# Four tiles gathered and four computed densely, where it was three and five: a retrieval layer re-split on one Trainium2 core

## The chip, the cores and the metric

The kernel runs on one core of a Trainium2 chip. The metric is the device time of one execution in microseconds (us). The kernel before took 2888.42 us (median of 3 runs, 2881.86 to 2891.72).

## The reference

The input is 1024 tokens of 1024 float32 channels. One layer first mixes tokens (two projections through `w_in` and `w_out`, a short convolution, a spatial gate) and adds the result to the input, giving `h`. Then it retrieves from 16384 single-neuron experts:

```
q    = (rmsnorm(h) @ w_q).reshape(t, 8, 2, 128)            # 8 heads, 2 halves
s    = einsum('thpd,hpkd->thpk', q, sub_keys)              # 128 keys per half
v1, i1 = top_k(s[:, :, 0], 16);  v2, i2 = top_k(s[:, :, 1], 16)
cand = v1[..., :, None] + v2[..., None, :]                 # 16 x 16 sums
cidx = i1[..., :, None] * 128 + i2[..., None, :]
top, pos = top_k(cand, 16);  idx = take(cidx, pos);  gates = softmax(top)
act  = gelu(einsum('thkd,td->thk', expert_u[idx], rmsnorm(h)))
y    = einsum('thk,thkd->td', gates * act, expert_v[idx])  # 8 x 16 experts per token
out  = rmsnorm(h + y)
```

## The kernel before

**Tiles.** The tokens are 8 tiles of 128. Tiles 0 to 3 are group A, tiles 4 to 7 group B. The front (`prep`, `mix`, `query`, `choose`) works on a group at a time. After it, the tiles of `S_TILES` (0, 6, 7) take the sparse path and those of `D_TILES` (1 to 5) the dense path.

**Front.** `mix` streams weight slices of 128 columns (`wide`, L230): each is loaded, split into a rounded part (ACT) and the rest (`split`, L169, on VectorE or one time in three on GpSimd), and multiplied in three products (`mm3`, L182: high by high, high by low, low by high). `query` (L365) does this for the 16 half-heads, and per half-head and tile VectorE searches the 16 largest of 128 scores (`top16`, L474). `choose` (L390) takes, per head, the 50 pairs of ranks that can be among the 16 largest sums (`NCAND`), adds scores on VectorE and indices on GpSimd, searches the 16 largest, and looks their indices up: compare 50 candidates with 16 positions (`eq`, L431, VectorE), multiply by the index (`sel_i`, L433, GpSimd), sum over the candidates (`idx`, L434, VectorE). For group A it is emitted after group B's `mix`; for group B it is interleaved with the queries for two tiles and put into the dense stage for the other two (`LATE`).

**Sparse path** (`sparse`, L510). A slot is one expert rank of one tile: GpSimd issues an indirect DMA that gathers 128 rows of 4 KB (`gx`, L522, 6 buffers), and VectorE consumes it, in a dot product with the token's row (L529) for `peer_u`, or in a multiply-add into `acc` (L538) for `peer_v`. A tile has 128 slots of each kind. It is emitted last and so has the lowest priority; the scheduler that orders each engine's instructions fills it into free time. `pace` (L501) holds it back: from slot `NFREE` = 70 on, each slot comes behind a given mark in VectorE's queue, and the marks are spread over the dense stage.

**Dense path.** `gates` (L549) builds, for each dense token, a 128 x 128 matrix of its gates by expert, from two one-hot matrices per token and a plain fp32 product, and stores it in device memory (`G_dr`). The one-hots are made on VectorE (`o2`, `o1`), the weighing `og` on GpSimd or ACT by the string `OGP`. `dense` (L595) then goes over 128 blocks of 128 experts. `up` multiplies the block's `peer_uT` with the tokens in two halves of 320 (`mm3`), applies Gelu, multiplies by the gates (L634), splits the product into `wh` and `wl` (L637, L638) and splits the block of `peer_v` too (L172, L173). `down` multiplies in three products per tile and half of the channels, over three blocks at a time: for two tiles into persistent PSUM banks, for three into a passing bank that VectorE adds to an accumulator (L651).

**Order.** Each engine runs its queue in order, as the scheduler wrote it. SyncE issues all DMAs but the gathers.

Of the kernel before, what the change touches and what calls it, by code (L numbers as in the profile page):

```python
# [29 lines left out]
NCAND = sum(NB)  # L30

S_TILES = [0, 6, 7]
D_TILES = [1, 2, 3, 4, 5]
GROUPS = [[0, 1, 2, 3], [4, 5, 6, 7]]
# [15 lines left out]
OGB = 2  # L50
O1B = 3
GPER = 3
GLAG = 0
LATE = [range(4, 28, 3), range(29, 61, 4)]
WRB = 2
CTB = 2
N1 = 45
N2 = 69
OGP = "GAAGA"
OGPB = "GA"  # L60
POOL_SPLIT = 1
NFREE = 70
PACE = 0.97


@with_exitstack
def block_kernel(ctx: ExitStack, tc: tile.TileContext, x, attn_g, w_in, conv_w, sgu_wT, sgu_b, sgu_g,
# [21 lines left out]
    dkx = ExitStack()  # L89
    dk = sb(dkx, "dk")  # L90
# [3 lines left out]
    X = [tk.tile([P, KC, 4 * P], F32R, name=n) for n in ("Xh", "Xl")]  # L94

    xt = sb(xtx, "xt")

    class Part:
        def __init__(self, pool, j0, n, late=()):
            self.pool, self.j0, self.n, self.late = pool, j0, n, late  # L100

    class Group:
        def __init__(self, tiles, dest, pool_share):
            self.tiles, self.dest, self.share = tiles, dest, pool_share
            self.nt = len(tiles)
            self.T = self.nt * P
            self.t0 = tiles[0] * P
# [44 lines left out]
    v_.tensor_copy(iota_c, iota_ki[:, 0:NCAND].unsqueeze(2).to_broadcast([P, NCAND, TOPK]))  # L152
# [13 lines left out]
    nsplit = [0]  # L166
    marks = []

    def split(pool, raw, shape, tag, bufs, eng=None):  # L169
# [60 lines left out]
    def wide(G, src, col, rh, rl, order=tuple(range(KC))):  # L230
        wh, wl = wslice(src, col, G.share)
# [5 lines left out]
    def mix(G):  # L237
# [112 lines left out]
        dt = [j for j, t in enumerate(tiles) if t in D_TILES]  # L350
        if dt:
            assert dt == list(range(dt[0], dt[-1] + 1))
            d0 = D_TILES.index(tiles[dt[0]])
            for i in range(2):
                nc.sync.dma_start(hd_dr[i, :, :, d0 * P:(d0 + len(dt)) * P],
                                  G.dest[i][:, :, dt[0] * P:(dt[-1] + 1) * P].bitcast(F32))
        st = [(j, t) for j, t in enumerate(tiles) if t in S_TILES]
        if st:
            gb = tk.tile([P, KC, P], F32, name="wraw", bufs=WRB).rearrange("p k c -> p (k c)")
            nc.sync.dma_start(gb, ffn_g.to_broadcast([P, D]))  # L360
            for j, t in st:
                gp_.tensor_tensor(hs[j], hs[j], gb, ALU.mult)
                nc.sync.dma_start(hn_dr[t * P:(t + 1) * P, :], hs[j])
# [26 lines left out]
    def choose(G, part):  # L390
        nt, late = part.n, part.late
        G, j0, tiles = part, 0, G.tiles[part.j0:part.j0 + part.n]
        for h in range(NH):
            if h:
                yield
            i1 = ks.tile([P, nt, TOPK], F32, name="i1")
            i = a_.activation(i1, G.ti[:, :, 2 * h, :], AF.Copy, scale=128.0)
            if late:
                after(i, marks[late[h]])
            i2 = ks.tile([P, nt, TOPK], F32, name="i2")  # L400
            i = a_.activation(i2, G.ti[:, :, 2 * h + 1, :], AF.Copy)
            if late:
                after(i, marks[late[h]])
            cand = ks.tile([P, nt, NCAND], F32, name="cand")
            cidx = ks.tile([P, nt, NCAND], F32, name="cidx")
            c = 0
            for a0, a1 in ((0, 1), (1, 2), (2, 3), (3, 4), (4, 5), (5, 8), (8, 16)):
                m, n = a1 - a0, NB[a0]
                for eng, dst, first, second in ((v_, cand, G.tv[:, :, 2 * h, :], G.tv[:, :, 2 * h + 1, :]),
                                                (gp_, cidx, i1, i2)):  # L410
                    if n == 1:
                        i = eng.tensor_tensor(dst[:, :, c:c + m], first[:, :, a0:a1],
                                          second[:, :, 0:1].to_broadcast([P, nt, m]), ALU.add)
                    elif m == 1:
                        i = eng.tensor_tensor(dst[:, :, c:c + n], second[:, :, 0:n],
                                          first[:, :, a0:a1].to_broadcast([P, nt, n]), ALU.add)
                    else:
                        i = eng.tensor_tensor(dst[:, :, c:c + m * n].rearrange("p j (a b) -> p j a b", b=n),
                                          second[:, :, 0:n].unsqueeze(2).to_broadcast([P, nt, m, n]),
                                          first[:, :, a0:a1].unsqueeze(3).to_broadcast([P, nt, m, n]), ALU.add)  # L420
                    if late:
                        after(i, marks[late[h]])
                c += m * n
            pos = ks.tile([P, nt, TOPK], U32, name="pos")
            for j in range(nt):
                top16(cand[:, j, :], G.top[:, j0 + j, h, :], pos[:, j, :])
            posf = ks.tile([P, nt, TOPK], BF16, name="posf")
            a_.activation(posf, pos, AF.Copy)
            for j in range(nt):
                eq = ks.tile([P, NCAND, TOPK], BF16, name="eq")  # L430
                v_.tensor_tensor(eq, iota_c, posf[:, j, :].unsqueeze(1).to_broadcast([P, NCAND, TOPK]), ALU.is_equal)  # L431
                sel_i = ks.tile([P, NCAND, TOPK], F32, name="sel_i")
                gp_.tensor_tensor(sel_i, eq, cidx[:, j, :].unsqueeze(2).to_broadcast([P, NCAND, TOPK]), ALU.mult)  # L433
                v_.tensor_reduce(G.idx[:, j0 + j, h, :], sel_i.rearrange("p c k -> p k c"), axis=AX.X, op=ALU.add)  # L434
# [339 lines left out]
```

## Time and profile before

| | |
|---|---|
| median of 3 runs | 2888.42 us |
| span of the profiled execution | 2884.6 us, 3.8 us under that median; the page gives no other time for it |
| TensorE (PE) busy | 2669.2 us, 93% |
| VectorE (DVE) busy | 2447.2 us, 85% |
| GpSimd (POOL) busy | 1422.3 us, 49% |
| ACT busy | 1045.3 us, 36% |
| DMA | 709.93 MB, 246 GB/s over the span |

Durations are of single instructions. Instructions of one engine overlap by their pipelines, so the step from one start to the next is what an engine really takes. The granted clock (PEclk) is a share of 2.4 GHz. The DMA share is the mean busy share of 16 DMA engines.

### The profile page before, as it was taken

The numbers are of one execution on the slowest core, as the hardware profiler recorded it, in microseconds if no ns is written. First come the engines' busy times: TensorE is split into PE (matmuls) and PEld (weight loads), VectorE is DVE, ScalarE is ACT, GpSimd is POOL, SyncE is SP. The second block draws the span as 40 slices with busy tenths as digits, with TensorE's granted clock in tenths as the row PEclk, the third lists the DMA queues.
The fourth block names the chain that finished last, engine by engine and source line by source line (L and its number), as shares of the span: only waits on it lengthen the run. The fifth ranks groups of instructions, "written<-read, shape, count | busy, mean of one in ns | idle before, by whom it ended". The sixth has DMA issues, their size and how long they took to land.

```text
span 2884.6 us, 40045 instructions
## 1 busy us (share of the span) xinstructions
PE 2669.2 (93%) x14243; PEld 2335.5 (81%) x14243; DVE 2447.2 (85%) x4792; ACT 1045.3 (36%) x1973; POOL 1422.3 (49%) x1192
## 2 busy tenths in 40 slices
PE   8997889778885789999999999999999999999998
PEld 6876667567774678888888988999998899899997
DVE  3337979969999869999999999998998888888994
ACT  5224242237765852222323322332323232232223
POOL 0102245644354536766666666655554555554540
PEclk9999978889997889999999999999999999999999
DMA  3225225466446778888889788888888988888881
GB/s 121 81 81 191 74 108 165 154 239 190 128 121 217 223 259 305 312 290 297 309 293 340 284 306 310 316 295 325 323 308 312 331 300 309 316 310 301 308 320 73
DMA packets 270360, 709.93 MB, mean 246 GB/s; under 512 B 21576, under 2 KB 112720, under 8 KB 269904
## 3 DMA queue, kind: packets, MB, share of 16 engines
q0 software_dynamic: 110592, 402.70, 39.7%
q1 hardware_dynamic: 159568, 304.67, 30.7%
q8 instruction: 112, 1.84, 0.3%
q14 instruction: 88, 0.72, 0.1%
HBM read 650.14 MB, written 57.15 MB: 245 GB/s over the span
## 4 chain that ended last, share of the span: by engine, by line
PE 42%; DVE 29%; issue 10%; POOL 6%; DMA 3%; ACT 2%; POOLq 0%; SPq 0%; DVEq 0%; ACTq 0%
PE pu L183 6%; PE pu L184 6%; PE pu L185 6%; DVE gx L529 4%; PE pv L183 4%; PE pv L185 4%; PE pv L184 4%; POOL gx L522 3%; PE pa L184 2%; PE pa L183 2%; PE pa L185 2%; DVE idx L434 2%; POOL sel_i L433 2%; DVE acc L538 2%; DVE a L634 2%
## 5 line engine op out<-in xcount | busy, mean ns | idle before, releaser
L522 POOL DMA_INDIRECT gx<-peer_v,si x384 | 522.8, 1361 | 406.6 <-DVE acc L538 290.3
L522 POOL DMA_INDIRECT gx<-peer_u,si x384 | 497.6, 1296 | 404.5 <-DVE dots L529 257.9
L183 PE MATMUL pu<-hD,uh 128*128 128x320 f32 x2048 | 634.7, 310 | 5.9 <-ACT a L633 5.1
L185 PE MATMUL pu<-hD,ul 128*128 128x320 f32 x2048 | 634.1, 310 | 0.0
L184 PE MATMUL pu<-hD,uh 128*128 128x320 f32 x2048 | 633.9, 310 | 0.0
L529 DVE CUSTOM_DVE_ANT_0 gx<-gx,hn 128x1024 f32<-128x1024 f32 x384 | 478.9, 1267 | 23.4 <-DMA gx<-peer_u,si 23.4
L538 DVE SCALAR_TENSOR_TENSOR acc<-gx,dots,acc 128x1024 f32<-128x1024 f32 x384 | 491.0, 1279 | 5.5 <-DMA gx<-peer_v,si 1.5
L183 PEld LDWEIGHTS pu<-hD,uh 128*128 128x128 f32 x2048 | 385.6, 188 | 9.1 <-ACT a L633 6.4
L184 PEld LDWEIGHTS pu<-hD,uh 128*128 128x128 f32 x2048 | 385.8, 188 | 1.9
L185 PEld LDWEIGHTS pu<-hD,ul 128*128 128x128 f32 x2048 | 385.6, 188 | 0.0
L172 ACT ACTIVATE vh<-raw 128x512 fp32r<-128x512 f32 x256 | 160.9, 633 | 495.5 <-PE pv L185 485.2
L183 PE MATMUL pv<-vh,wh 128*128 128x512 f32 x768 | 304.2, 396 | 27.7 <-DVE ac L651 26.0
L185 PE MATMUL pv<-vh,wl 128*128 128x512 f32 x768 | 302.1, 393 | 3.8 <-DVE wl L638 3.8
L637 ACT ACTIVATE wh<-a 128x320 fp32r<-128x320 f32 x256 | 120.9, 472 | 506.5 <-DVE a L634 493.4
L184 PE MATMUL pv<-vl,wh 128*128 128x512 f32 x768 | 301.1, 392 | 0.0
L185 PE MATMUL pp<-Xh,wl 128*128 128x512 f32 x576 | 242.1, 421 | 20.2 <-DVE wl L173 11.0
L576 PE MATMUL pt<-og,o 128*128 128x128 f32 x1280 | 209.4, 317 | 42.4 <-POOL og L566 25.2
L634 DVE TENSOR_TENSOR a<-a,G 128x320 f32<-128x320 f32 x256 | 186.3, 728 | 72.6 <-ACT a L633 70.8
L183 PE MATMUL pp<-Xh,wh 128*128 128x512 f32 x576 | 242.7, 422 | 3.4 <-ACT wh L172 3.3
L184 PE MATMUL pp<-Xl,wh 128*128 128x512 f32 x576 | 241.8, 420 | 0.0
L576 PEld LDWEIGHTS pt<-og,o 128*128 128x128 f32 x1280 | 184.7, 219 | 68.2 <-POOL og L566 30.0
L173 DVE TENSOR_TENSOR vl<-raw,vh 128x512 fp32r<-128x512 f32 x256 | 173.7, 696 | 41.0 <-ACT vh L172 40.7
(187 smaller groups left out, 4795.0 us busy)
## 6 DMA issues: line engine op xcount, KB each, us to landing
raw<-peer_uT SPq DMA_DIRECT2D x128, 512.0 KB
raw<-peer_v SPq DMA_DIRECT2D x128, 512.0 KB
G_dr<-stg SPq DMA_DIRECT2D x20, 2048.0 KB
G<-G_dr SPq DMA_DIRECT2D x64, 640.0 KB
wraw<-w_in SPq DMA_DIRECT2D x40, 512.0 KB
wraw<-w_q SPq DMA_DIRECT2D x32, 512.0 KB
xt<-x SPq DMA_DIRECT2D x16, 512.0 KB
wraw<-w_out SPq DMA_DIRECT2D x16, 512.0 KB
```

The costliest lines, as they stand in the source:

```text
L172: a_.activation(hi, raw, AF.Copy)
L173: (eng or v_).tensor_tensor(lo, raw, hi.bitcast(F32), ALU.subtract)
L183: pe.matmul(o, lh, rh, start=first, stop=False)
L184: pe.matmul(o, lh, rl, start=False, stop=False)
L185: pe.matmul(o, ll, rh, start=False, stop=last)
L433: gp_.tensor_tensor(sel_i, eq, cidx[:, j, :].unsqueeze(2).to_broadcast([P, NCAND, TOPK]), ALU.mult)
L522: gp_.indirect_dma_start(out=gx, out_offset=None, in_=tab, in_offset=bass.IndirectOffsetOnAxis(ap=ii[:, s:s + 1], axis=0))
L529: pace(v_.tensor_tensor_reduce(gu, gu, hn, 1.0, 0.0, ALU.mult, ALU.add, dots[:, s:s + 1]), slot[0])
L538: pace(v_.scalar_tensor_tensor(acc, gv, dots[:, s:s + 1], acc, op0=ALU.mult, op1=ALU.add), slot[0])
L576: pe.matmul(o[:, i, :], o2[:, m, :], og[:, m, :], start=True, stop=True)
L634: gm = v_.tensor_tensor(a, a, Gt[hf][:, :, c % CB], ALU.mult)
L637: a_.activation(wh[:, sl], a, AF.Copy)
```

## The change

`S_TILES` becomes 0 to 3 (group A) and `D_TILES` 4 to 7 (group B). In detail:

- `choose` is emitted between the queries of its own group, one head behind two half-heads, for A and for B; nothing of it is left for the dense stage. The look-up is split by rank: the first 8 results are looked for among 20 candidates, the other 8 among all 50, for two tiles in one instruction, and the product moves from GpSimd to VectorE. Indices and gates of two heads at a time are handed to the sparse path.
- `NFREE` becomes 150, and the conditions for earlier slots (`N1`, `N2`) go. There are 1024 slots.
- The weight split is always on VectorE. The normalised rows `hn` of tiles 0 to 3 are multiplied on VectorE.
- `gates` runs after all of group B's selection, for 64 blocks of 8 tokens: three of four weigh on ACT, every fourth has VectorE make and weigh `og` in one instruction per token. The first 12 `up`s are emitted between them.
- `up` works on 512 tokens at once and writes Gelu's result into a ring of 4 groups of 4 expert blocks, stored `[P, 512, 4]`; the gates multiply a whole group in one instruction. The result is not split, and `peer_v` is not: `down` is one plain fp32 product per block, tile and half, over 4 blocks. Five of the eight accumulators persist in PSUM, three are `LOOSE`.
- The tokens of group B stay in SBUF (`X`); the copy through `hd_dr` goes.

```diff
-S_TILES = [0, 6, 7]
-D_TILES = [1, 2, 3, 4, 5]
+FIRST = [(0, 1, 0, 8), (1, 2, 0, 4), (2, 4, 0, 2), (4, 8, 0, 1)]
+REST = [(0, 1, 8, 8), (1, 2, 4, 4), (2, 3, 2, 3), (3, 4, 2, 2), (4, 5, 1, 2), (5, 8, 1, 1), (8, 16, 0, 1)]
+S_TILES = [0, 1, 2, 3]
+D_TILES = [4, 5, 6, 7]
-OGP = "GAAGA"
-NFREE = 70
+OGP = "AAAT"
+NFREE = 150
+LOOSE = [(0, 0), (0, 1), (1, 0)]
+ORDER = [(0, 0), (2, 0), (0, 1), (2, 1), (1, 0), (3, 0), (3, 1), (1, 1)]
...
     def choose(G, part):
...
-                gp_.tensor_tensor(sel_i, eq, cidx[:, j, :].unsqueeze(2).to_broadcast([P, NCAND, TOPK]), ALU.mult)
+            for k0, nc_ in ((0, NFIRST), (8, NCAND)):
+                shape = [P, nt, nc_, 8]
...
+                v_.tensor_tensor(eq, iota_c[:, 0:nc_, k0:k0 + 8].unsqueeze(1).to_broadcast(shape),
+                                 posf[:, :, k0:k0 + 8].unsqueeze(2).to_broadcast(shape), ALU.is_equal)
...
+                v_.tensor_tensor(sel, eq, cidx[:, :, 0:nc_].unsqueeze(3).to_broadcast(shape), ALU.mult)
+                v_.tensor_reduce(part.idx[:, :, h, k0:k0 + 8], sel.rearrange("p j c k -> p j k c"), axis=AX.X,
+                                 op=ALU.add)
...
     def gates(pool, tiles, n0, n1, who):
...
+                    for m in range(OB):
+                        v_.tensor_scalar(og[:, m, :], iota_k, d[:, 0, tl + m:tl + m + 1],
+                                         d[:, 2, tl + m:tl + m + 1], op0=ALU.is_equal, op1=ALU.mult)
...
+        def up(self, c, pspool, tag, bufs):
+            g, m = divmod(c, CB)
+            if m == 0:
+                self.ring[g] = self.rp.tile([P, TD, CB], F32, name="ring", bufs=RING)
+            raw = self.up_.tile([P, KC, P], F32, name="uraw", bufs=RB)
+            nc.sync.dma_start(raw, peer_uT[c])
+            uh, ul = split(self.up_, raw, [P, KC, P], "u", 2)
+            o = pspool.tile([P, TD], F32, name=tag, bufs=bufs)
+            for k in range(KC):
+                mm3(o, uh[:, k, :], ul[:, k, :], X[0][:, k, :], X[1][:, k, :], k == 0, k == KC - 1)
+            a_.activation(self.ring[g][:, :, m], o, AF.Gelu)
...
+            for g in range(NG):
+                Gt = pool.tile([P, TD, CB], F32, name="G", bufs=GB)
+                nc.sync.dma_start(Gt, G_dr[:, g, :, :])
+                w = self.ring.pop(g)
+                marks.append(v_.tensor_tensor(w, w, Gt, ALU.mult))
...
+                if g + RING - 1 < NG:
+                    for m in range(CB):
+                        self.up((g + RING - 1) * CB + m, pps, "pu", 2)
+                for j, dh in ORDER:
+                    loose = (j, dh) in LOOSE
+                    o = pps.tile([P, 512], F32, name="pv", bufs=1) if loose else self.accs[j, dh]
+                    for m in range(CB):
+                        pe.matmul(o, w[:, j * P:(j + 1) * P, m], vs[m][:, dh * 512:(dh + 1) * 512],
+                                  start=m == 0 and (loose or g == 0), stop=m == CB - 1 and (loose or g == NG - 1))
+                    if loose:
+                        dst = self.full[j][:, dh * 512:(dh + 1) * 512]
+                        marks.append(v_.tensor_tensor(dst, dst, o, ALU.add))
...
+        qa = query(A, sb(c1, "pqA"))
+        ca = [choose(A, part) for part in A.parts]
+        for h in range(NH):
+            take(qa, 2)
+            for ch in ca:
+                take(ch, 1)
...
+        gg = gates(sb(c1, "gp"), D_TILES, 0, NTB, OGP)
+        for c in range((RING - 1) * CB):
+            dn.up(c, ps, "pp", 4)
+            take(gg, 64 // ((RING - 1) * CB))
```

## Rows read from the trace of the kernel before

**Rows 1.** The page: busy us of each engine, share of the span, instructions.
```profile
PE 2669.2 (93%) x14243; PEld 2335.5 (81%) x14243; DVE 2447.2 (85%) x4792; ACT 1045.3 (36%) x1973; POOL 1422.3 (49%) x1192
```
**Rows 2.** Windows: stretch, its length, busy us by engine, clock, DMA share, GB/s.
```profile
0.00:243.00 243.00, 220.78 (x1004) 176.59 (x1004) 89.04 (x160) 95.83 (x143) 27.18 (x18) 0.94 0.33 104
243.00:366.00 123.00, 106.57 (x494) 86.12 (x494) 119.61 (x627) 40.17 (x70) 31.27 (x48) 0.93 0.36 115
366.00:645.00 279.00, 233.31 (x972) 182.29 (x971) 231.70 (x562) 93.96 (x166) 147.66 (x164) 0.85 0.49 167
645.00:932.00 287.00, 224.28 (x1282) 189.61 (x1280) 268.68 (x877) 187.22 (x412) 131.66 (x111) 0.90 0.54 162
932.00:1046.00 114.00, 90.34 (x512) 77.82 (x512) 91.28 (x83) 90.96 (x198) 62.55 (x28) 0.84 0.73 229
1046.00:1800.00 754.00, 723.47 (x3999) 650.51 (x4000) 696.21 (x1140) 217.17 (x421) 473.56 (x403) 0.99 0.86 304
1800.00:2600.00 800.00, 794.63 (x4454) 722.78 (x4454) 722.56 (x1047) 234.83 (x418) 439.65 (x341) 1.00 0.87 314
```
**Rows 3.** Groups of VectorE instructions: busy us, mean ns, idle before and its releaser.
```profile
L538 DVE SCALAR_TENSOR_TENSOR acc<-gx,dots,acc 128x1024 f32<-128x1024 f32 x384 | 491.0, 1279 | 5.5 <-DMA gx<-peer_v,si 1.5
L529 DVE CUSTOM_DVE_ANT_0 gx<-gx,hn 128x1024 f32<-128x1024 f32 x384 | 478.9, 1267 | 23.4 <-DMA gx<-peer_u,si 23.4
L634 DVE TENSOR_TENSOR a<-a,G 128x320 f32<-128x320 f32 x256 | 186.3, 728 | 72.6 <-ACT a L633 70.8 <-DMA G<-G_dr 1.7
L651 DVE TENSOR_TENSOR ac<-ac,pv 128x512 f32<-128x512 f32 x258 | 175.3, 679 | 12.5 <-PE pv L185 12.5
L173 DVE TENSOR_TENSOR vl<-raw,vh 128x512 fp32r<-128x512 f32 x256 | 173.7, 696 | 41.0 <-ACT vh L172 40.7 <-DMA G_dr<-stg 0.3
L173 DVE TENSOR_TENSOR ul<-raw,uh 128x1024 fp32r<-128x1024 f32 x128 | 157.2, 1228 | 19.3 <-ACT uh L172 19.3
L638 DVE TENSOR_TENSOR wl<-a,wh 128x320 fp32r<-128x320 f32 x256 | 124.1, 485 | 6.7 <-ACT wh L637 6.7
```
**Rows 4.** Timeline of PE in two places: start us, us, instruction, count.
```profile
733.42 3.51 PE L576 MATMUL pt<-og,o 128*128 128x128 f32 x30
...
2000.64 0.39 PE L183 MATMUL pv<-vh,wh 128*128 128x512 f32 x1
...
2016.28 0.31 PE L183 MATMUL pu<-hD,uh 128*128 128x320 f32 x1
...
2019.80 0.31 PE L183 MATMUL pu<-hD,uh 128*128 128x320 f32 x1
```
**Rows 5.** The page's groups: weight loads of the fp32 product, and gathers.
```profile
L576 PEld LDWEIGHTS pt<-og,o 128*128 128x128 f32 x1280 | 184.7, 219 | 68.2 <-POOL og L566 30.0
L522 POOL DMA_INDIRECT gx<-peer_v,si x384 | 522.8, 1361 | 406.6 <-DVE acc L538 290.3
```
**Rows 6.** Timeline of VectorE in the queries: first and last of one half-head's search.
```profile
283.57 0.48 DVE L475 MAX8 tv<-s 128x8 f32<-128x128 f32 x2
...
288.25 1.47 DVE L434 TENSOR_REDUCE idx<-sel_i 128x16 f32<-128x800 f32 x1
```
**Rows 7.** Groups of VectorE in the selection.
```profile
L434 DVE TENSOR_REDUCE idx<-sel_i 128x16 f32<-128x800 f32 x64 | 97.4, 1522 | 40.0 <-POOL sel_i L433 40.0
L431 DVE TENSOR_TENSOR eq<-iota_c,posf 128x800 bf16<-128x800 bf16 x64 | 44.8, 700 | 0.8 <-ACT posf L428 0.8
```
**Rows 8.** Groups of ACT from 932 to 1046 us, where 32 blocks of gates run alone.
```profile
L571 ACT ACTIVATE og<-o,dT 128x128 f32<-128x128 bf16 x128 | 57.7, 519 | 1.0 <-DVE o L561 1.0
L578 ACT ACTIVATE stg<-pt 128x512 f32<-128x512 f32 x64 | 37.8, 591 | 22.0 <-PE pt L576 21.5
```
**Rows 9.** One window of 20 us, columns as in rows 2; and the page's gather queue.
```profile
2460.00:2480.00 20.00, 18.83 (x85) 15.30 (x84) 15.92 (x27) 3.91 (x7) 10.65 (x8) 1.00 1.02 410
...
q0 software_dynamic: 110592, 402.70, 39.7%
```
**Rows 10.** Timeline of VectorE at the end: the last add of a passing bank.
```profile
2871.92 0.69 DVE L651 TENSOR_TENSOR ac<-ac,pv 128x512 f32<-128x512 f32 x1
```

More of the change, by code (lines that the diff above doesn't have):

```diff
@@ L390, in choose @@
     def choose(G, part):
-        nt, late = part.n, part.late
-        G, j0, tiles = part, 0, G.tiles[part.j0:part.j0 + part.n]
-        for h in range(NH):
[L394 to L405, printed above, removed]
+        nt = part.n
@@ L427, in choose @@
[L427 removed]
+                top16(cand[:, j, :], part.top[:, j, h, :], pos[:, j, :])
+            posf = ks.tile([P, nt, TOPK], BF16, name="posf", bufs=2)
             a_.activation(posf, pos, AF.Copy)
[L429 to L432, printed above, removed]
[L433 to L434 removed]
@@ new lines, in choose @@
+            if h % 2:
+                hs = slice(h - 1, h + 1)
+                if sparse_:
+                    for j, t in enumerate(tiles):
+                        v_.tensor_copy(idx_of[t][:, (h - 1) * TOPK:(h + 1) * TOPK].rearrange("p (h k) -> p h k", h=2),
+                                       part.idx[:, j, hs, :])
+                for j in range(nt):
+                    gf, tf = gt[:, j, hs, :], part.top[:, j, hs, :]
+                    v_.tensor_tensor(gf, tf, tf[:, :, 0:1].to_broadcast([P, 2, TOPK]), ALU.subtract)
+                gh = gt[:, :, hs, :]
+                a_.activation(gh, gh, AF.Exp)
+                den = ks.tile([P, nt, 2], F32, name="den", bufs=2)
+                v_.tensor_reduce(den, gh, axis=AX.X, op=ALU.add)
+                v_.reciprocal(den, den)
+                v_.tensor_tensor(gh, gh, den.unsqueeze(3).to_broadcast([P, nt, 2, TOPK]), ALU.mult)
@@ L691, in block_kernel @@
     with ExitStack() as c1:
-        take(query(A, sb(c1, "pqA")))
+        qa = query(A, sb(c1, "pqA"))
[4 more added lines that the diff above has]
+                take(ch, 1)
+        for ch in ca:
+            take(ch)
     load_x(B)
@@ L695, in block_kernel @@
     mix(B)
[L696 to L699 removed]
     xtx.close()
     with ExitStack() as c1:
[L702 to L725 removed]
+        qb = query(B, sb(c1, "pqB"))
+        cb = [choose(B, part) for part in B.parts]
+        for h in range(NH):
+            take(qb, 2)
+            for ch in cb:
+                take(ch, 1)
+        for part, ch in zip(B.parts, cb):
+            take(ch)
+            spread(B, part)
+    tks.close()
+    kdx.close()
+    rx = ExitStack()
+    dn = Dense(sb(rx, "ringp", side="right"), sb(rx, "uvp", side="right"))
+    with ExitStack() as c1:
+        gg = gates(sb(c1, "gp"), D_TILES, 0, NTB, OGP)
+        for c in range((RING - 1) * CB):
+            dn.up(c, ps, "pp", 4)
+            take(gg, 64 // ((RING - 1) * CB))
+        take(gg)
     pre.close()
@@ L730, in block_kernel @@
         pps = c2.enter_context(tc.tile_pool(name="pps", bufs=2, space=PSUM))
-        dense(pool, up_, pacc, pps, D_TILES, hD, u0)
+        dn.run(pool, pacc, pps)
         sparse(spool, S_TILES)
```

362 lines of the change are left out of this document (121 added, 241 removed).

## Prediction

> **What bounds the kernel now.** I read the busy table first, then windows by stage, then the groups and timelines of the stage that is longest. The busy table puts PE at 93% and VectorE at 85% [rows 1], but these are means over different stages [rows 2]. Up to 243 us group A's mixing fills PE; from 243 to 366, in A's queries, VectorE is full (119.6 of 123); from 366 to 645 both are busy with B's mixing and A's selection; from 645 to 932 VectorE again (268.7 of 287), with queries, selection and half of the gates; 932 to 1046 is the rest of the gates. The dense stage runs from 1046 to the end: in its steady part PE is busy 794.6 of 800 us, while the DMA engines are 87% busy at 314 GB/s and VectorE 90%. So the dense stage is bound by PE, the front mostly by VectorE, and the front leaves DMA at 33 to 54%. The change takes PE work out of the dense stage, puts DMA work in, and lengthens the front. Which of these decides is the question.
>
> All sums are made against the profiled span of 2884.6 us, which lies 3.8 us under the median of the runs.
>
> **Up to 243 us.** The weight split leaves GpSimd for VectorE, which is busy 89 of 243 us there; PE is busy 221 [rows 2]. Cost nothing; -10 to +5 us.
>
> **A's queries with selection.** This is now one stretch on VectorE.
> - A search of one half-head over four tiles goes from 283.57 to 288.25, 4.68 us [rows 6]; 16 are 75 us.
> - 16 weight splits at the price of `ul`, 1.23 us [rows 3]: 20 us. Four `hn` products at the same price: 5 us.
> - Selection, per head and pair of tiles, 16 times. The look-up handles 2 x (20 + 50) x 8 = 1120 places, where it was 2 x 800. Compare: 2 x 0.70 x 0.7 = 0.98 us; sum: 2 x 1.52 x 0.7 = 2.13 us [rows 7]; the product, new on VectorE, at the fp32 price of `ul` (1.2 ns a place): 1.34 us. Small adds and the search over 50 sums: 2.6 us, an estimate a little over the 2.34 us that half of a 128-score search takes; softmax 0.3. Together 7.35 us, times 16: 118 us.
>
> That is 218 us of work. At the 97% that VectorE reached in the same stretch [rows 2] it is 225 us, where it was 123. Below, 190 if the short instructions overlap as they partly do now; above, 275 if the chains through ACT and GpSimd leave holes. A's stretch ends at 468.
>
> **B's mixing.** It was 279 us, with A's selection as filler; A's own, without filler, was at most 243 [rows 2]. Now the filler is the first gather slots, 1.26 us each ((491.0 + 478.9) / 768 [rows 3]), which run only where VectorE is free. I take 255, less 10 because B starts while A's last selection runs; bounds 228 and 279. End: 713.
>
> **B's queries with selection.** The same 213 us of work without `hn`: 220, and 8 for the hand-over to the gates. End: 941. These two stretches stand on the path, and hide under nothing.
>
> **Gates.** 64 blocks; ACT sets the pace. 128 weighings took 57.7 us, so 16 blocks cost 3.6 us each; 48 blocks are 173 us. Copies out of PSUM: 128 x 0.59 = 76 us [rows 8]. Sum 249 us, I take 250: bounds 228 (the rate of 932 to 1046 us, 114 us for 32 blocks) and 290 (12 `up`s that also fall on ACT, and waits). The first 12 `up`s use PE's idle time. End: 1191, so the dense stage begins 145 us later than before.
>
> The slots: VectorE has in 243 to 1191 some 948 us, and 218 + 213 + 90 (B's mixing, as much as A's) + 183 (gates, twice the 91 us of the 32 blocks in rows 2) = 704 us of other work; 150 slots are 190 us and fit. So 874 of the 1024 slots are left for the dense stage; before, 698 of 768.
>
> **Dense stage, three engines.**
> - PE. Between 2000.64 and 2016.28 us PE starts 69 products of 512 columns, 0.227 us each, and up to 2019.80 24 of 320, 0.147 each. A plain fp32 product appears as two passes; 30 passes of 128 columns took 3.51 us, so 0.111 us each without the last one's latency of about 0.3 [rows 4]. At 2.4 GHz that is two clocks a column (0.107 us) and some 4 ns. For 512 columns I take 4 x 0.107 us and 4 ns: 0.431 us. Per group of four blocks: 4 x 24 x 0.227 + 64 x 0.431 = 21.8 + 27.6 = 49.4 us. 32 groups less the 12 early `up`s (65 us): 1515 us. Before, per four blocks: 4 x (48 x 0.147 + 30 x 0.227) = 55.5 us.
> - VectorE: 874 x 1.26 = 1101; `ul` 116 x 1.23 = 143; gates' products 32 x 2.5 = 80 (2048 values at the price of `ul`); loose adds 96 x 0.68 = 65; the ends of eight tiles, about 3 us each, 25. Sum 1414 us. The splits `vl` and `wl` (173.7 and 124.1) are gone, and L651 falls from 258 to 96 [rows 3].
> - DMA. A slot moves 402.70 MB / 768 = 0.524 MB [rows 9]. 874 slots: 458 MB; `peer_uT` 116 x 0.524 = 61, `peer_v` 67, gates 33.6, the rest 8. Sum 628 MB. To move it in PE's 1515 us would take 415 GB/s; the best 20 us that I show reach 410 with all engines busy [rows 9], the steady stage 314 at a share of 0.87 [rows 2].
>
> So DMA becomes the bound. Between 314 / 0.87 = 361 (no faster packets when the queue is full) and 410 (always full and fast) I take 383, halfway: in the fast windows the share is full, and six gather buffers keep about 3 MB asked for, but VectorE's other work comes in lumps. 628 / 383 = 1640 us; bounds 1546 (PE at 98%) and 1740. GpSimd, 874 gathers at 1.36 us [rows 5], needs 1189 us and is hidden.
>
> **Two rules.** The row of 20 us shows 410 GB/s with PE, VectorE and gathers at work [rows 9]. The Trainium skill, "DMA: Bandwidth & Descriptors", section "Where 436 GB/s comes from", gives about 358 GB/s as what binds transfers between device memory and SBUF for one core. By it the stage would take 628 / 358 = 1754 us; the trace does not agree in that window, and the rule stands beside rival 1 below.
>
> The down product reads its weights with a stride of four floats. VectorE's read of the gates with that stride took 728 ns for 320 values, where a contiguous one took 485 [rows 3]: 1.5 times. The Trainium skill, "SBUF — State Buffer", section "Door 1: The DMA port swizzle", says that SBUF works in lines of 16 bytes and that each access to a new line pays. The trace agrees in kind; what it does to weight loads no row shows.
>
> At 1.5 times, a load of 219 ns [rows 5] is 329 ns and stays under the 431 of a pass.
>
> **Sum.** 243 + 225 + 245 + 228 + 250 + 1640 + 12 (from the last add to the end, as now: 2872.6 to 2884.6 [rows 10]) = 2843 us; with the 3.8 to the median, 2847. I forecast 2845 us, 1.5% faster.
>
> **Rivals.**
> 1. *Slower: the DMA engines stay at 361 GB/s.* 1191 + 1740 + 12 = 2943, 2947 as a median. For it: the long-run share and rate of rows 2. Against: rows 9. It decides from 628 / (2884.6 - 1191 - 12) = 373 GB/s down.
>    The 358 GB/s of the Trainium skill's page on DMA would give 2961.
> 2. *PE stays the bound* because transfers reach over 400 GB/s: 1191 + 1546 + 12 + 4 = 2753. For it: windows at 410; against: VectorE's order is fixed, and a stalled slot holds up `ul`.
> 3. *The selection is a chain*, 275 us in each group: +100 us, 2945. For it: `eq` waits for ACT, the index for GpSimd. Against: 97% busy before, with two pairs of tiles and searches to fill in.
> 4. *The change does not do what it says:* only some 75 slots run before the dense stage, since the scheduler finds no room. 39 MB more at 383 GB/s: +102 us, 2947.
> 5. *Strided weight loads* over 2.3 times as long: from 0.51 us a pass on, 2048 passes eat the gain; at three times, 2048 x (0.657 - 0.431) = +463 on PE, 3175.
>
> **Chances.** Forecast 0.46 (dense stage at 370 to 395 GB/s, 2797 to 2904), rival 1 0.17, rival 2 0.20, rival 3 0.09, rival 4 0.05, rival 5 0.03. No change is within 0.3% (9 us), about what a measurement of this kernel can tell. Most of the forecast's own range and rival 2 are faster: 0.63; its upper end gives 0.08 for the same; the rest, 0.29, is slower. The range, 2735 to 2970, takes in rivals 1 to 4.
>
> **What would show it.** In the profile after: selection stretches of about 225 us with VectorE over 95%; the first group's gate product near 1200 us; some 150 slots before it; in the dense stage a DMA share over 0.95 at 375 to 395 GB/s, PE at 90 to 95% with waits for VectorE, VectorE with waits for gathers. Two passes of 0.43 us per down product. PE at 98% would be rival 2; a DMA share near 1 at 360 GB/s rival 1; weight loads longer than a pass rival 5. I am wrong if the dense stage begins before 1130 or after 1260 us, or if its length is not set by transfers.

## The result: 2.5% slower, by the transfers of the dense stage

The kernel after takes 2959.05 us (median of 4 runs, 2950.23 to 2972.07) against 2890.07 for the kernel before in the same comparison: ratio 1.0248, 95% interval 1.0212 to 1.0285. The forecast was 2845 us. The profiled execution has a span of 2948.5 us, 10.6 under that median.

Page of the kernel after, busy us by engine and the gather queue (answers to [rows 1, 9]):

```profile
PE 2491.7 (85%) x9120; PEld 1916.8 (65%) x9120; DVE 2278.2 (77%) x4500; ACT 794.3 (27%) x1312; POOL 1372.4 (47%) x1383
...
q0 software_dynamic: 147456, 536.94, 49.6%
```

Every compute engine has less to do than in [rows 1], and the gathers have more (536.94 MB for 402.70 in [rows 9]); TensorE's share falls from 93% to 85%, VectorE's from 85% to 77%. No engine is full, and the kernel is slower: time is spent waiting.

Windows by stage of the kernel after, columns as in [rows 2]. The first window keeps the 243 us of [rows 2], though the first product of a query with its keys comes at 236 here (243 before). The later stages end at 458, 701, 932 and 1182 us; the last dense product ends at 2923:

```profile
0.00:243.00 243.00, 221.80 (x1041) 180.62 (x1042) 105.52 (x228) 96.52 (x144) 0.88 (x7) 0.95 0.32 111
243.00:458.00 215.00, 107.28 (x481) 83.81 (x480) 214.32 (x1051) 55.80 (x117) 54.25 (x193) 0.76 0.27 90
458.00:701.00 243.00, 217.02 (x944) 173.27 (x945) 198.11 (x301) 82.25 (x121) 137.82 (x101) 0.87 0.83 301
701.00:932.00 231.00, 133.88 (x592) 106.09 (x591) 230.28 (x1085) 58.37 (x125) 57.31 (x194) 0.77 0.26 87
932.00:1182.00 250.00, 225.44 (x1237) 183.28 (x1236) 169.58 (x264) 242.62 (x533) 24.57 (x21) 0.93 0.64 190
1182.00:1400.00 218.00, 193.79 (x616) 146.13 (x615) 167.04 (x169) 33.65 (x34) 128.58 (x99) 0.95 0.99 382
1400.00:1800.00 400.00, 365.16 (x1123) 275.31 (x1122) 304.48 (x388) 61.97 (x64) 250.62 (x197) 0.95 0.96 354
1800.00:2200.00 400.00, 367.77 (x1132) 276.88 (x1132) 310.99 (x363) 61.68 (x65) 254.00 (x200) 0.95 0.96 359
2200.00:2600.00 400.00, 363.61 (x1122) 273.45 (x1121) 307.40 (x358) 61.72 (x64) 248.15 (x200) 0.95 0.95 357
2600.00:2923.00 323.00, 295.97 (x845) 217.96 (x843) 252.19 (x281) 35.45 (x39) 210.58 (x171) 0.96 0.94 346
```

The front took what was forecast: VectorE is busy 214.3 of 215 us in A's selection stretch and 230.3 of 231 in B's, ACT 242.6 of 250 in the gates. The dense stage has no full engine: PE 91%, VectorE 77%, but the DMA share 0.95 to 0.96 at 354 to 359 GB/s. It lasts 1741 us (1182 to 2923) where 1640 were forecast; before, counted to the last dense product too, it lasted 1831 (1046 to 2877):

```profile
2876.48 0.39 PE L185 MATMUL pa<-vh,wl 128*128 128x512 f32 x1
```

So the front gave away 136 us, the dense stage gave back 90, and the end, 26 us from the last product to the end of the span where it was 8, took 18: +64, the difference of the two spans.

Gathers that GpSimd started in the first four stages from 243 us on (count in brackets):

```profile
243.00:458.00 215.00, 24.47 (x17) 0.76 0.27 90
458.00:701.00 243.00, 137.82 (x101) 0.87 0.83 301
701.00:932.00 231.00, 27.45 (x18) 0.77 0.26 87
932.00:1182.00 250.00, 24.57 (x21) 0.93 0.64 190
```

One that spans a boundary is in two windows, so they are 156: the forecast's 150 early slots, and six more gathers issued ahead into the six buffers.

Groups of the kernel after (columns as in [rows 3]; the last one is idle time ahead of the group, and what ended it). The first two answer to L538 and L529 in [rows 3], the weight load to [rows 5]:

```profile
L522 DVE SCALAR_TENSOR_TENSOR acc<-gx,dots,acc 128x1024 f32<-128x1024 f32 x512 | 658.0, 1285 | 127.7 <-DMA gx<-peer_v,si 117.9
L513 DVE CUSTOM_DVE_ANT_0 gx<-gx,hn 128x1024 f32<-128x1024 f32 x512 | 613.8, 1222 | 171.8 <-DMA gx<-peer_u,si 168.6
L181 PE MATMUL pu<-Xh,ul 128*128 128x512 f32 x928 | 391.9, 422 | 127.7 <-DVE ul L170 127.7
L620 PEld LDWEIGHTS pa<-v,ring 128*128 128x128 f32 x1280 | 394.6, 308 | 154.8
```

VectorE waited 286 us for gathered rows, 25 us before. TensorE in turn waited 128 us for VectorE's split `ul`. One place where a late row stops TensorE, VectorE first (start us, us, instruction; in brackets the idle time ahead of it and its releaser):

```profile
1983.56 1.23 DVE L513 CUSTOM_DVE_ANT_0 gx<-gx,hn 128x1024 f32<-128x1024 f32 x1 [0.93 <-DMA gx<-peer_u,si]
1986.87 1.22 DVE L513 CUSTOM_DVE_ANT_0 gx<-gx,hn 128x1024 f32<-128x1024 f32 x1 [2.08 <-DMA gx<-peer_u,si]
1989.43 1.23 DVE L513 CUSTOM_DVE_ANT_0 gx<-gx,hn 128x1024 f32<-128x1024 f32 x1 [1.33 <-DMA gx<-peer_u,si]
1991.81 1.22 DVE L513 CUSTOM_DVE_ANT_0 gx<-gx,hn 128x1024 f32<-128x1024 f32 x1 [1.14 <-DMA gx<-peer_u,si]
...
1995.75 1.21 DVE L170 TENSOR_TENSOR ul<-uraw,uh 128x1024 fp32r<-128x1024 f32 x1
```

then ACT:

```profile
1993.08 0.23 ACT L516 ACTIVATE dots<-dots 128x32 f32<-128x32 f32 x1 [37.88 <-DVE dots L513]
1993.21 1.04 ACT L169 ACTIVATE uh<-uraw 128x1024 fp32r<-128x1024 f32 x1
1994.16 1.08 ACT L590 ACTIVATE ring<-pu 128x512 f32<-128x512 f32 x1
```

and TensorE beside them:

```profile
1991.16 0.39 PE L180 MATMUL pu<-Xl,uh 128*128 128x512 f32 x1
1991.39 0.40 PE L181 MATMUL pu<-Xh,ul 128*128 128x512 f32 x1
1995.29 0.50 PE L179 MATMUL pu<-Xh,uh 128*128 128x512 f32 x1 [3.51 <-ACT ring L590]
1995.63 0.40 PE L180 MATMUL pu<-Xl,uh 128*128 128x512 f32 x1
1997.02 0.79 PE L181 MATMUL pu<-Xh,ul 128*128 128x512 f32 x1 [0.98 <-DVE ul L170]
1997.61 0.63 PE L179 MATMUL pu<-Xh,uh 128*128 128x512 f32 x1
1998.04 0.63 PE L180 MATMUL pu<-Xl,uh 128*128 128x512 f32 x1
```

Two queues in a fixed order pass the wait on. On ACT, Gelu of the sparse path's `dots` stands ahead of `uh` and of the dense path's Gelu `ring`, and it waits for the last dot product of 32; only `ring` empties the bank (`pu`) that TensorE needs next, hence the stop of 3.51 us. On VectorE, `ul` stands behind the dot products that wait for rows, hence the stop of 0.98 us. So a row that lands late stops TensorE. The 128 us are 28 such stops for `ul` in the dense stage, about one per group of four blocks; within each and the 8 us ahead of it VectorE stood 2.5 to 6.9 us for rows. Stops for `ring` are 8 us in all. The idle time is not all of it. Windows of the same place:

```profile
1985.00:1995.00 10.00, 6.79 (x30) 5.25 (x28) 5.36 (x10) 1.92 (x3) 6.17 (x7) 1.00 1.03 411
1995.00:1999.70 4.70, 3.42 (x8) 2.45 (x9) 4.70 (x8) 2.07 (x3) 4.09 (x3) 0.62 1.02 392
1999.70:2002.70 3.00, 3.00 (x8) 2.31 (x7) 3.00 (x6) 0.00 (x0) 2.70 (x2) 0.50 0.99 367
2002.70:2010.50 7.80, 7.80 (x34) 6.36 (x33) 3.50 (x5) 2.07 (x3) 6.57 (x5) 0.99 0.88 302
```

In the stretch that holds the end of the first stop and the second, the granted clock is 0.62 on average, then 0.50, which is 1.2 GHz; a product of 512 columns takes 0.43 us from start to start (1997.61 to 1998.04) where it took 0.23 (1991.16 to 1991.39). Only from 2002.7 on is it 0.99 again. Over the dense stage the mean is 0.95, before it was 0.99 to 1.00 [rows 2].

### The profile page after: what moved, and what is told of

Read it like the earlier page. It is cut to its first block, busy times and chain, and to the rows that moved or that the text cites. A ratio compares the mean times of both kernels' runs of the same rounds, so it can differ in the third digit from the quotient of the medians.

```text
span 2948.5 us, 29181 instructions
## 1 busy us (share of the span) xinstructions
PE 2491.7 (85%) x9120; PEld 1916.8 (65%) x9120; DVE 2278.2 (77%) x4500; ACT 794.3 (27%) x1312; POOL 1372.4 (47%) x1383
## 3 DMA queue, kind: packets, MB, share of 16 engines
q0 software_dynamic: 147456, 536.94, 49.6%
## 4 chain that ended last, share of the span: by engine, by line
issue 41%; POOL 17%; DVE 16%; PE 14%; DMA 11%; ACT 0%; POOLq 0%; SPq 0%; DVEq 0%; ACTq 0%
POOL gx L506 17%; DMA gx<-peer_v,si 8%; PE pp L181 3%; PE pp L179 3%; PE pp L180 3%; DMA gx<-peer_u,si 2%; DVE idx L430 2%; DVE acc L522 1%; DVE gx L513 1%; DVE sel L429 1%; DVE s L472 1%; DVE ti L474 1%; DVE ti L471 1%; DVE wl L170 1%; DVE tv L470 1%
## 5 line engine op out<-in xcount | busy, mean ns | idle before, releaser
L513 DVE CUSTOM_DVE_ANT_0 gx<-gx,hn 128x1024 f32<-128x1024 f32 x512 | 613.8, 1222 | 171.8 <-DMA gx<-peer_u,si 168.6
L620 PE MATMUL pa<-v,ring 128*128 128x512 f32 x1280 | 565.0, 592 | 0.0
L181 PE MATMUL pu<-Xh,ul 128*128 128x512 f32 x928 | 391.9, 422 | 127.7 <-DVE ul L170 127.7
L620 PEld LDWEIGHTS pa<-v,ring 128*128 128x128 f32 x1280 | 394.6, 308 | 154.8
L179 PE MATMUL pu<-Xh,uh 128*128 128x512 f32 x928 | 397.1, 428 | 11.9 <-ACT ring L590 7.7
L180 PE MATMUL pu<-Xl,uh 128*128 128x512 f32 x928 | 383.0, 413 | 0.0
L620 PE MATMUL pv<-v,ring 128*128 128x512 f32 x768 | 348.6, 597 | 15.4 <-DVE ac L624 15.4
L181 PEld LDWEIGHTS pu<-Xh,ul 128*128 128x128 f32 x928 | 188.7, 203 | 182.6 <-DVE ul L170 140.0
L620 PEld LDWEIGHTS pv<-v,ring 128*128 128x128 f32 x768 | 234.0, 309 | 107.5 <-DVE ac L624 21.1
L170 DVE TENSOR_TENSOR ul<-uraw,uh 128x1024 fp32r<-128x1024 f32 x128 | 156.2, 1222 | 105.0 <-ACT uh L169 79.3
L179 PEld LDWEIGHTS pu<-Xh,uh 128*128 128x128 f32 x928 | 188.9, 204 | 56.3 <-ACT ring L590 8.6
L180 PEld LDWEIGHTS pu<-Xl,uh 128*128 128x128 f32 x928 | 187.3, 202 | 49.9 <-issue 6.7
L565 PE MATMUL pt<-og,o 128*128 128x128 f32 x1024 | 185.0, 318 | 20.1 <-ACT og L556 19.3
```

The costliest lines, as they stand in the source:

```text
L170: v_.tensor_tensor(lo, raw, hi.bitcast(F32), ALU.subtract)
L179: pe.matmul(o, lh, rh, start=first, stop=False)
L180: pe.matmul(o, lh, rl, start=False, stop=False)
L181: pe.matmul(o, ll, rh, start=False, stop=last)
L513: pace(v_.tensor_tensor_reduce(gu, gu, hn, 1.0, 0.0, ALU.mult, ALU.add, dots[:, s:s + 1]), slot[0])
L565: pe.matmul(o[:, i, :], o2[:, m, :], og[:, m, :], start=True, stop=True)
```

## The experiments

Three theories: **T**, transfers set the dense stage, and the DMA engines move no more than about 357 GB/s; **P**, TensorE sets it; **B**, transfers set it, but because six gather buffers cannot keep the queues full (a buffer must be consumed, refilled and landed before its next use), B+ if that is most of it. All ratios are to the kernel before, which ran beside them each time (medians of 2887 to 2891 us); microseconds "less than after" are against the 2959.05 us above.

**1. Half the down product**, two of each four blocks.

```diff
-                    for m in range(CB):
+                    for m in (0, CB - 1):
                         pe.matmul(o, w[:, j * P:(j + 1) * P, m], vs[m][:, dh * 512:(dh + 1) * 512],
```

> The changed kernel, with the down product of only blocks 0 and 3 of each group of four (half of the product is left out), everything else and all transfers kept. Its PE work in the dense stage falls by 32 products x 2 passes... that is 16 of 32 products a group, 16 x 0.86 = 13.8 us, 441 us in all. Theory T (transfers at about 357 GB/s set the dense stage, 1182 to 2922 us): no change, 2930 to 2975 us. Theory P (PE, busy 91% there, sets it): some 300 to 440 us less.

Measured 2904.69 us, ratio 1.0034 [1.0000, 1.0069]: 54 us less than the kernel after, where 1024 passes of 0.43 us, 440 us of TensorE work, were taken away. P falls; but T, which expected at least 2930, misses too, by 25 us. Windows, the second after TensorE's last product, when only gathers are left:

```profile
1400.00:2540.00 1140.00, 984.28 (x3188) 704.29 (x3189) 912.65 (x1066) 208.92 (x216) 721.17 (x558) 0.93 0.98 372
2560.00:2880.00 320.00, 0.00 (x0) 0.00 (x0) 261.99 (x303) 0.69 (x3) 255.21 (x208) 0.50 0.94 341
```

The gathers alone, 208 in 320 us, step by 1.54 us: a buffer comes round in 6 x 1.54 = 9.2 us. VectorE is not full (262 of 320), GpSimd's issue is not (255 of 320), and 341 GB/s is less than was moved with the other queue at work. In the kernel after, 595 gathers start from 1400 to 2600: 2.02 us each, a round of 12.1 us. In the first window here they are 558 in 1140 us, 2.04 us each: with TensorE relieved, the six buffers bring in rows no faster, and the step from 357 to 372 GB/s comes from the other queue.

**2. Half of `peer_v` not loaded:** odd blocks reuse the block before, 33.5 MB less.

```diff
                 for m in range(CB):
+                    if m % 2:
+                        vs.append(vs[-1])
+                        continue
```

> The changed kernel, with only every second block of peer_v loaded and used twice (so the output is that of other weights). 64 x 0.524 = 33.5 MB less of 628 MB, the same work on every engine. Theory T: 33.5 / 0.357 = 94 us less, about 2865 us. Theory P: no change. Theory B (the round trip of the six gather buffers sets the slot rate): gathers wait a little less in the queues, 0 to 40 us less.

Measured 2858.26 us, ratio 0.9881 [0.9830, 0.9933]: 101 us less than after, with TensorE's and VectorE's work unchanged. Transfers set the stage; at 358 GB/s 33.5 MB are 94 us, as T expected. B's 0 to 40 us are missed: the bytes of either queue cost time. Its window, at a share of 0.97 and 361 GB/s, has 637 gathers, one in 1.88 us where it was 2.02:

```profile
1400.00:2600.00 1200.00, 1143.67 (x3627) 862.59 (x3626) 984.29 (x1184) 201.34 (x209) 804.98 (x637) 0.98 0.97 361
```

**3. Seven gather buffers.**

```diff
-NGX = 6
+NGX = 7
```

> The changed kernel with seven gather buffers for six. Theory T: the engines are 96% busy already, at most 1% less (2930 to 2960 us). Theory B: one slot more in each round trip, up to 16% more slots a microsecond, until PE stops it: 100 us or more less. Theory P: no change.

Measured 2922.57 us, ratio 1.0113 [1.0083, 1.0142], 36 us less than after: more than T allows, less than B expected. Its window, which answers to the three of after from 1400 to 2600 us (there 357 GB/s):

```profile
1400.00:2600.00 1200.00, 1115.87 (x3476) 840.89 (x3475) 949.52 (x1128) 189.97 (x197) 765.45 (x615) 0.96 0.97 367
```

**4. More early slots.**

```diff
-NFREE = 150
+NFREE = 230
```

> The changed kernel with 230 free slots for 150. In the profile all 150 free slots were done at 1046 us, and from there to 1182 us, while the gates are made, VectorE and the transfers have room. Theory T: some 60 to 80 slots more run there, 31 to 42 MB less for the dense stage: 88 to 117 us less there, less 10 to 30 us by which the gates get longer; 2860 to 2900 us in all. Theory P: no change or slower.

Measured 2985.33 us, ratio 1.0324 [1.0286, 1.0362]: slower by 26 us than after, the other way from what was expected. Gathers started by 1182 us were 174 instead of 156, 18 more and not 60 to 80: the marker was not what held most of the slots back. The first gates' product moved from 1201 to 1222 us, and later the rate fell:

```profile
1400.00:1800.00 400.00, 365.86 (x1115) 271.24 (x1115) 325.59 (x392) 56.07 (x58) 280.63 (x217) 0.95 0.99 375
1800.00:2200.00 400.00, 363.30 (x1122) 273.67 (x1121) 287.34 (x341) 61.44 (x64) 230.03 (x182) 0.95 0.91 334
```

A share of 0.91 means that fewer gathers were asked for; whether the marks, now spread over fewer slots, do it was not tried by itself. In the first of the two windows the same six buffers bring in 217 gathers, one in 1.84 us: the number of buffers does not fix the rate alone, the places of the slots in VectorE's queue count too.

**5. Ten gather buffers in the dense stage**, from slot 160 on.

```diff
-                gx = pool.tile([P, D], F32, name="gx", bufs=NGX)
+                if slot[0] >= 160 and slot[0] % 10 >= 6:
+                    gx = more.tile([P, D], F32, name="gy", bufs=4)
+                else:
+                    gx = pool.tile([P, D], F32, name="gx", bufs=NGX)
...
-        sparse(spool, S_TILES)
+        sparse(spool, S_TILES, sb(c2, "more"))
```

> The changed kernel with four more gather buffers once slot 160 is reached, ten in all in the dense stage. With seven it was 36 us faster than with six. Theory T (the engines' rate is reached): no more than another 10 us, 2910 to 2960 us. Theory B+ (a round trip of 12 us over six buffers leaves the queues empty between VectorE's lumps): the rate goes from 357 towards the 390 GB/s of the first 200 us of the stage, 628 / 0.39 = 1610 us for 1740, so 2830 to 2890 us.

Measured 2867.60 us, ratio 0.9926 [0.9905, 0.9947]: 91 us less than after, and faster than the kernel before. The same window:

```profile
1400.00:2600.00 1200.00, 1126.42 (x3534) 851.35 (x3534) 958.42 (x1154) 193.84 (x201) 778.26 (x624) 0.97 0.98 374
```

In the source nothing but the buffers was changed, and the DMA engines move 374 GB/s where they moved 357. T falls, B+ stands. One thing comes along: the scheduler writes VectorE's order anew, and in the dense stage it is not that of the kernel after (nor is it with five or seven buffers), so buffers and order were not told apart. The order did not get smoother: the longest run of slots with no split, gates' product or loose add between is 14 here, 12 in the kernel after.

**6. Three gathered tiles.**

```diff
-            k = int((n - NFREE) * len(marks) * PACE / (len(S_TILES) * 2 * P - NFREE))
+            k = int((n - NFREE) * len(marks) * PACE / (3 * 2 * P - NFREE))
...
-        sparse(spool, S_TILES)
+        sparse(spool, S_TILES[:3])
...
```

> The changed kernel with only tiles 0 to 2 on the sparse path (tile 3's retrieval is left out and h is written for it), 768 slots spread over the same dense stage. 134 MB less, 494 MB in the dense stage. Theory T: transfers would take 494 / 0.357 = 1384 us, so PE becomes the bound with its 1515 us: dense stage 1530 to 1580 us, 2730 to 2780 us in all. If instead the PE work is longer than I worked out (plain fp32 dearer than 0.43 us a pass, or weight loads in the way), the stage stays over 1600 us.

Measured 2810.18 us, ratio 0.9729 [0.9704, 0.9753], 55 over the middle of the first expectation; its alternative, a stage of over 1600 us, came out. The dense stage lasts from 1184 to 2799, 1615 us, and in it TensorE is full:

```profile
1400.00:2600.00 1200.00, 1160.32 (x3686) 878.57 (x3686) 772.82 (x897) 198.32 (x201) 570.54 (x459) 0.98 0.84 304
```

With transfers out of the way (304 GB/s) TensorE sets 1615 us, at 97% busy and a granted clock of 0.98; the forecast's bound was 1546. TensorE is busy for 1548 us of the stage, 0.98 x 1548 = 1517 at the full clock, so its work (1515) was sized right; the bound left 31 us for idle time and clock, and the idle time alone is 67, 54 of it waits for `ul`.

**7. A quarter of the gates' blocks weighed on GpSimd.**

```diff
-OGP = "AAAT"
+OGP = "AGAT"
...
+                elif who[nblk % len(who)] == "G":
+                    o1 = pool.tile([P, P, OB], BF16, name="o1", bufs=2)
+                    v_.tensor_tensor(o1, iota_r, db[:, tl:tl + OB].unsqueeze(1).to_broadcast([P, P, OB]),
+                                     ALU.is_equal)
+                    gp_.tensor_tensor(og.rearrange("p t c -> p c t"), o1,
+                                      d[:, 2, tl:tl + OB].unsqueeze(1).to_broadcast([P, P, OB]), ALU.mult)
```

> The changed kernel with every fourth block of gates weighed on GpSimd for ACT, so that two of four stay on ACT. ACT's work per four blocks falls from 3 x 3.6 + 4 x 1.19 = 15.6 to 12.0 us, 58 us over the stage from 930 to 1182 us. If ACT sets that stage: 40 to 60 us less in all, 2900 to 2920 us. If VectorE or GpSimd's gathers set it: no change.

Measured 2938.67 us, ratio 1.0172 [1.0155, 1.0189]. That is half of what was expected if ACT set the gates' stage, where ACT is now busy 190 us of 213. The dense stage began 25 us earlier (1157), and 20 us came through by the medians (their ranges allow some 10 more or less). In the two profiled executions the stage behind it is 23 us longer (1764 us), at 354 GB/s from 1400 to 2600, and the spans differ by 2 us: how much of the gain survives is not settled by this run.

**8. Both edits, 5 and 7.**

> Ten gather buffers and the gates partly on GpSimd together. The two stages lie behind each other, so the gains add: under theory B+ and ACT as the gates' bound 2780 to 2850 us, under theory T 2890 to 2920 us.

Measured 2835.10 us, ratio 0.9810 [0.9790, 0.9830]: within the first expectation and 32 us under experiment 5. The dense stage begins at 1150 instead of the 1186 of experiment 5, so with ten buffers 32 of these 37 us come through. From 1400 to 2600 us the rate is 374 GB/s, as in experiment 5: the gates' edit leaves it alone.

**9 and 10. The kernel before with five and with seven buffers.**

```diff
-NGX = 6
+NGX = 5
```
```diff
-                gx = pool.tile([P, D], F32, name="gx", bufs=NGX)
+                if slot[0] >= 80 and slot[0] % 7 >= 6:
+                    gx = more.tile([P, D], F32, name="gy", bufs=1)
+                else:
+                    gx = pool.tile([P, D], F32, name="gx", bufs=NGX)
...
```

> The kernel before with five gather buffers in place of six. Theory (the number of gather buffers limits the rate only where VectorE consumes a slot as soon as it lands): in the kernel before, TensorE sets the dense stage and landed rows wait for VectorE some 6 us of a 15 us round, so five buffers cost almost nothing: 2880 to 2905 us, ratio 0.997 to 1.006. Rival (the buffers always set the pace of the dense stage, whatever the kernel): a slot of 2.50 us becomes 3.0, +0.5 x 698 = +350 us at most; anything over +60 us, 2950 and up, speaks for it.

> The kernel before with a seventh gather buffer in the dense stage. Theory: no change, within 0.4% (2878 to 2898 us), since its transfers were not late. Rival (more buffers help in every kernel, so that the gain of the ten-buffer run says nothing of the change): 1% faster or more, as the seventh buffer gave in the kernel after.

Measured 2926.64 us, ratio 1.0117 [1.0100, 1.0134], and 2889.73, ratio 0.9984 [0.9965, 1.0002], against 2891.08 for six. The seventh buffer gives nothing there, as expected; taking the sixth away costs 36 us, where at most 14 were expected. With six the kernel before was just past the bend, not far from it: its window with five shows 304 GB/s, with six it was 311.

```profile
1400.00:2600.00 1200.00, 1167.70 (x6479) 1052.99 (x6478) 1079.32 (x1628) 345.73 (x632) 693.22 (x548) 1.00 0.86 304
```

**11. The kernel after with five buffers** (the one-line edit of 9).

> The kernel after with five gather buffers in place of six. Theory (round trip over the number of buffers): a slot took 2.02 us with six buffers; the round of 12.1 us shortens a little where the queues are emptier, down to the 9.3 us measured with gathers alone, so a slot takes 1.9 to 2.4 us, and the dense stage grows by 40 to 200 us: 3000 to 3150, likeliest near 3040. Rival (the DMA engines' own limit of about 357 GB/s sets the stage, buffers are enough): within 15 us of 2959.

Measured 3030.30 us, ratio 1.0489 [1.0472, 1.0507], 71 us over the kernel after, near the 3040 expected; the rival, the engines' own limit, falls. But the step to the next gather is 2.08 us and not 2.4: the round of a buffer shortened to 10.4 us. Its window:

```profile
1400.00:2600.00 1200.00, 1072.82 (x3268) 803.62 (x3268) 900.04 (x1067) 178.91 (x186) 746.82 (x576) 0.94 0.94 346
```

**12. Eleven buffers** (in 5, `% 11` and five of them), and the gates of 7.

> Eleven gather buffers in the dense stage, with a quarter of the gates' blocks weighed on GpSimd, against ten of them with the same gates (2835 us). Theory: with ten buffers the share of the DMA engines is already 0.976 at 374 GB/s, so an eleventh gives little: 2822 to 2838. If buffers were still what limits (twelve us of round over the number of buffers), one tenth more would give up to -60 us: 2775 to 2810, and TensorE's floor of some 1600 us would be next.

Measured 2813.95 us, ratio 0.9731 [0.9715, 0.9747]: the fastest version, 21 us under experiment 8. It lies between the two expectations, 8 us below the one and 4 above the other.

```profile
1400.00:2600.00 1200.00, 1141.43 (x3582) 863.02 (x3581) 971.38 (x1177) 192.22 (x199) 801.24 (x636) 0.97 0.99 380
```

The DMA share is 0.99, and the dense stage takes 1642 us, 27 over the 1615 of experiment 6 that TensorE sets. More than eleven buffers were not tried.

The buffers in the kernel after, by the profiled executions but for the medians. The stage is the dense one, from the last gates to the last product; rates and steps are those of 1400 to 2600 us; a round is buffers x step; the last column is the median from issue to landing of all gathers of the run (the trace of the run with seven does not hold it).

| buffers | median us | stage us | GB/s | DMA share | granted clock | one gather in us | round us | to landing us |
|---|---|---|---|---|---|---|---|---|
| 5 | 3030 | 1808 | 346 | 0.94 | 0.94 | 2.08 | 10.4 | 6.6 |
| 6 | 2959 | 1741 | 357 | 0.96 | 0.95 | 2.02 | 12.1 | 7.1 |
| 7 | 2923 | 1709 | 367 | 0.97 | 0.96 | 1.95 | 13.7 | - |
| 10 | 2868 | 1666 | 374 | 0.98 | 0.97 | 1.92 | 19.2 | 8.9 |
| 10, gates of 7 | 2835 | 1672 | 374 | 0.98 | 0.97 | 1.93 | 19.3 | 8.7 |
| 11, gates of 7 | 2814 | 1642 | 380 | 0.99 | 0.97 | 1.89 | 20.8 | 8.9 |

The 623 MB of the stage over these rates are 1801, 1745, 1698, 1666, 1666 and 1639 us, the measured stages within 1%: the rate sets the length. From five to eleven buffers the rate grows by a tenth, and the round doubles: a further buffer mostly waits.

## Why the prediction was wrong

**The step that failed** is the rate of the dense stage: "Between 314 / 0.87 = 361 (no faster packets when the queue is full) and 410 (always full and fast) I take 383, halfway: in the fast windows the share is full, and six gather buffers keep about 3 MB asked for". The bytes were right (the windows sum to 623 MB from 1182 to 2923 us, 628 forecast for the stage and its end), the rate was not: 623 / 1741 = 358 GB/s, 25 less. That is the 101 us, and it turned a forecast of 1.5% faster into 2.5% slower. The prediction's own break-even rate, 373 GB/s, lies between six and ten buffers: with ten the engines move 374, and the kernel is 0.7% faster than the one before.

The premise about six buffers was the error, and [rows 9] could not have carried it: 20 us of a full queue show what the engines can do, not what six buffers can keep up. A buffer is asked for only part of its round, the time from issue to landing. In the kernel after (min, median, max):

```profile
DMA to landing us min/median/max: 4.2/7.1/13.8
```

and with eleven buffers:

```profile
DMA to landing us min/median/max: 4.3/8.9/17.7
```

At one gather in 2.02 us, 7.1 us are 3.5 buffers or 1.8 MB asked for at a time, not 3 MB; with eleven buffers, at 1.89 us, they are 4.7 buffers or 2.5 MB. With these the engines reach 380 GB/s, about the forecast's 383. Of the 26 GB/s between 383 and 357 some 15 are share (0.96 for 1) and 11 are speed at a given share (357 / 0.96 = 372 for 383). More buffers raised both, with VectorE's order rewritten along with them (experiment 5); why packets move faster with more asked for, no run shows.

Matched gather by gather (means, 1400 to 2600 us, the 521 of 595 gathers whose landing the trace of after holds), the round of 12.1 us is 7.5 from issue to landing, 1.8 until VectorE takes the row, 1.25 for its work and 1.5 until the next issue. Half of the rows are taken within 0.4 us of landing: VectorE takes most rows as soon as they are there. With eleven buffers the four parts are 9.4, 5.9, 1.25 and 4.3 us.

The kernel before hid the limit. Gathers that it started in the dense stage (count in brackets):

```profile
1046.00:1800.00 754.00, 390.77 (x289) 0.99 0.86 304
1800.00:2600.00 800.00, 426.90 (x323) 1.00 0.87 314
```

612 in 1554 us are one in 2.54 us, because TensorE, full there, set the pace; VectorE waited only 25 us for rows in the whole run [rows 3]. In the runs of the kernel before with five and with seven buffers a landed row waits 3.6 and 8.1 us for VectorE. The change asks for one gather in 1640 / 874 = 1.88 us, and six buffers gave one in 2.02.

**Rival 1's number, not its mechanism.** 2947 was its time, 1740 its stage; 2959 and 1741 came out. But it said that the engines stay at 361 GB/s, packets being no faster in a full queue. Experiments 5 and 12 move 374 and 380 over 1200 us with the same packets, experiment 1 moves 372 over 1140 us with six buffers, and the kernel after itself moved 382 in the first 218 us of its dense stage. The Trainium skill, "DMA: Bandwidth & Descriptors", section "Where 436 GB/s comes from", names about 358 GB/s as what binds one core's transfers with device memory. The kernel after would fit that by chance; the runs with more buffers do not agree.

**What held** (forecast, then measured in brackets). A's mixing to 243 (236); A's selection to 468 (458); B's mixing to 713 (701); B's selection to 941 (932); gates to 1191 (1182); 150 early slots (150). A plain fp32 pass: 0.431 us forecast; the timeline shows eight passes from 2010.52 to 2013.95, 0.429 each.

```profile
2010.52 3.60 PE L620 MATMUL pv<-v,ring 128*128 128x512 f32 x8
2013.95 3.60 PE L620 MATMUL pa<-v,ring 128*128 128x512 f32 x8
```

The strided weight loads of rival 5 take 308 ns against 219 [rows 5], 1.41 times, and stay under the pass. The Trainium skill, "SBUF — State Buffer", section "Door 1: The DMA port swizzle", has each access to a new 16-byte line pay; the trace agrees in kind. (The 3175 us of rival 5 do not follow from its own numbers: 2845 + 1515 + 463 - 1640 = 3183.) Rivals 3 and 4 fell with the front. Rival 2 fell too: transfers did not pass 400 GB/s but in short stretches, and its 1546 us for TensorE is 69 short of experiment 6.

**The end**, 12 us, was 26, counted from the last product: the last gathered slots run after it (VectorE starts its last two multiply-adds from 2937.8 us on). The forecast counted from the last add of a passing bank [rows 10], 4 us ahead of the last product there; before, 8 us lie behind that product.

The sum of the errors: -9 at the front, +101, +14 make +106 on the forecast span of 2843; 2948.5 was measured.

## What to carry to other kernels

Count what a gather stream keeps asked for: not all its buffers, but the part of a buffer's round (free, issued, landed, consumed) between issue and landing, here 3.5 of six. Before work is moved from an engine to transfers, do not size them by the peak of a short window, in which everything is asked for; where landed data waits for its consumer before the change, the limit does not show. The round is no constant to divide by the number of buffers: it went from 10.4 to 20.8 us as they went from five to eleven, for a tenth more rate. With eleven buffers and lighter gates the same change is 2.7% faster than the kernel before.

## What the runs showed of the hardware

- Gathers alone, six buffers of 0.524 MB, reach 341 GB/s at a share of 0.94; with the second queue at work, 357; with eleven buffers, 380 at 0.99. With more asked for, the same packets moved faster at a given share: 346 / 0.94 = 368 with five buffers, 357 / 0.96 = 372 with six, 380 / 0.99 = 384 with eleven.
- After a stop of 3.5 us, and around a second one of 1.0 us, TensorE's granted clock fell to 0.50 and was back at 0.99 from 2002.7 us on, 7.4 us after the first stop ended. A late row so costs TensorE twice: the wait, and products at 0.43 instead of 0.23 us.
- Leave for 80 more early slots put in 18 and made the kernel slower (experiment 4), with a lower DMA share in the middle of the dense stage.
